# One encoder layer on one core: the first four rows of x loaded together with their weights, three output tiles in one pass, the last product's banks primed with the residual, and the copies of turned probabilities tied

## The chip, the cores and the metric

The kernel runs on 1 core of one Trainium2 chip. The metric is the time of one execution on the device in microseconds (us). The times of a kernel are the median of its runs; a profile is one further execution with the hardware profiler on.

## The reference

One layer over 512 positions of width 2048, in float32. With `xn = rms_norm(x)`:

```
proj = xn @ w_in                    # 2048 x 5120: u_val, u_gate, q, k, v
y_conv = silu(layer_norm(depthwise_conv31(u_val * sigmoid(u_gate))))
y_na   = softmax(q k / 8 + bias) v  # 16 heads of 64, window 8 x 16 on an 8 x 64 grid
x = x + [rms_norm(y_conv), rms_norm(y_na)] @ w_out
up = depthwise_conv3(rms_norm(x) @ w_up);  gate, val = split(up)      # 2 x 5632
x = x + (silu(gate) * val) @ w_down
out = rms_norm(x)
```

## The kernel before

Every matrix product is made at more than half precision of float32 from two rounded parts: a weight tile `raw` is copied by ScalarE (ACT) to a high part `whi` (L133), and VectorE (DVE) makes the low part `wlo = raw - whi` (L134). The activations are split in the same way (`xh`, `xl`). One block of 128 x 128 weights then costs three matmuls over 512 positions: hi x hi, hi x lo, lo x hi (L150, L151, L153). `parts` makes the pair and keeps four of each (NW = 4); `weights` (L172) hands out the next pair and keeps three made ahead (AHEAD = 3). A pair is a "unit" of 8 blocks, so 24 matmuls.

The work of TensorE (PE) runs in this order:

- **Filler.** 11 matmuls on a tile of ones (WARM, L122), which the profile counts as 22.
- **First GLU** (`first_glu`, L357). The value and gate tiles of channel block 0, side by side in two banks, while x comes in. The weights for this come in an order of their own, `w_0`: for each of the 16 rows of x (128 channels by 512 positions), the two blocks that it multiplies. Rows 0 and 1 are loaded alone on SyncE's queue (SP, L289), and their weights on ScalarE's queue (L109), together with the factors `g1` (L104). Later rows come in pairs (L294), and their weights in pieces of 2 or 4 rows (`cuts`, `piece`). `split_x` makes `xh` and `xl` with the factor of the norm on ACT (L270) and DVE (L271). `pin` keeps these instructions in the order written. Behind this stage x is loaded again with positions on the partitions (`xn`, L306) for the sums of squares (L312).
- **Projections.** Channel blocks 1 to 7 (two tiles each) and 8 pairs of heads (three tiles each), mixed by ORDER. Behind them DVE runs the 31 taps of the depthwise convolution, at most four behind each `wlo`. `attend` makes a pair's attention as steps, of which `tick` runs one behind each unit: scores, softmax, then `turn` (TensorE turns the probabilities, L517, bank `trp`), `turned_p` (ACT copies them out as `pt`, L525), then `values` (L534, in the bank `po`). The convolution branch is finished during head pairs 5 and 6; its last root is made in the bank `po` too, and ACT copies it out as `ra` (L254).
- **Output product, gated MLP** (L641 to L860): as a seven-product scheme over halves.
- **Last product** (`product2`, L874), seven products over `TURN2`, four banks each. The last is c = 5 for output rows 0 to 255 and columns 0 to 1023. Its last four units are held back (TAIL), and each bank is finished by itself. Then `ready` (L930) adds the bank to `e3`, the residual with all earlier products (L936), squares it on ACT (L938) and multiplies by the last norm's factor (L940); `all_but_one` and `write` make the root and scale and store the rows.

A scheduler chooses the order of the instructions on each engine by priorities in the order of the program; `shifted` moves a priority, and `issue_after(i)` puts what it holds behind the instruction i.

Of the kernel before, what the change touches and what calls it, by code (L numbers as in the profile page):

```python
# [16 lines left out]
P = 128  # L17
# [17 lines left out]
U = 8  # L35
# [14 lines left out]
WARM = 11  # L50
# [26 lines left out]
def layer(ctx: ExitStack, tc: tile.TileContext, xT, xn, w_0, w_in, w_out, w_up, w_down, par, tab, g3, out):  # L77
# [26 lines left out]
    nc.scalar.dma_start(g1, par[:, :KD])  # L104
    cuts = (0, 1, 2, 4, 8, 12, 16)
    first = []
    for k0, k1 in zip(cuts[:3], cuts[1:4]):
        first.append(t2("we")[:, :2 * (k1 - k0) * P])
        nc.scalar.dma_start(first[-1], w_0[:, 2 * k0 * P:2 * k1 * P])  # L109
# [20 lines left out]
    def parts(raw, n):  # L130
        hi = wpool.tile([P, U * P], F32R, tag="whi", name="whi", bufs=NW)
        lo = wpool.tile([P, U * P], F32R, tag="wlo", name="wlo", bufs=NW)
        i = nc.scalar.activation(hi[:, :n], raw[:, :n], AF.Copy)  # L133
# [10 lines left out]
    tight, taps = [], []  # L144
# [123 lines left out]
    def split_x(k, x):  # L268
        h, l = t2("xh", F32R), t2("xl", F32R)
        pin(nc.scalar.activation(h, x, AF.Copy, scale=g1[:, k:k + 1]))  # L270
        pin(nc.vector.scalar_tensor_tensor(l, x, g1[:, k:k + 1], h.bitcast(F32), op0=ALU.mult, op1=ALU.subtract))  # L271
        xs.append((h, l))

    def piece(raw, k0, k1):
        if k1 - k0 > 2:
            raw, i = raw_unit(w_0[:, 2 * k0 * P:2 * k1 * P], 2 * (k1 - k0) * P)
            pin(i)
            w = parts(raw, 2 * (k1 - k0) * P)
        else:
            w = t2("weh", F32R)[:, :2 * (k1 - k0) * P], t2("wel", F32R)[:, :2 * (k1 - k0) * P]  # L280
            w += nc.scalar.activation(w[0], raw, AF.Copy), nc.vector.tensor_sub(w[1], raw, w[0].bitcast(F32))
        pin(w[2])
        pin(w[3])
        return k0, k1, w[0], w[1]

    pieces, early = [], []
    for k in range(2):
        x = t2("x")
        pin(nc.sync.dma_start(x, xT[0][:, k * S:(k + 1) * S]))  # L289
        split_x(k, x)  # L290
        pieces.append(piece(first[k], k, k + 1))
    for p, at in ((1, 2), (2, 3), (3, 0), (4, 4), (5, 0), (6, 5), (7, 0)):
# [4 lines left out]
        if at:  # L297
            pieces.append(piece(first[2] if at == 2 else None, cuts[at], cuts[at + 1]))
    squares = sm.tile([P, S // P, 2], F32, tag="ss", name="ss")
    for u in range(2):  # L300
        raw, i = raw_unit(w_in[NC_ + 1, :, u * U * P:(u + 1) * U * P], U * P)
        pin(i)
        for t in range(2 * u, 2 * u + 2):
            for i in range(2):
                x = t4([P, D // 2], "xn")
                pin(nc.sync.dma_start(x, xn[t * P:(t + 1) * P, i * D // 2:(i + 1) * D // 2]))  # L306
                if t == 2 * u and i == 0:
                    w = parts(raw, U * P)
                    pin(w[2])
                    pin(w[3])  # L310
                    early.append(w[:2])
                pin(nc.scalar.activation(x, x, AF.Square, accum_out=squares[:, t, i:i + 1]))  # L312
    last = pin(nc.sync.dma_start(prm, par))
    for i in range(6):
        plan.append(lambda i=i: early[i - 4] if i > 3 else None)
# [6 lines left out]
    del plan[6:12]  # L322
# [5 lines left out]
    def stats1():  # L328
        for _ in range(3):
# [20 lines left out]
    ys, ypair = [], []  # L350

    def glu(i):
        pg, pv = project(NC_ + i), project(i)
# [3 lines left out]
    def first_glu():  # L357
        two = [psa.tile([P, S], F32, tag="tr", name="pj", bufs=2) for _ in range(2)]
        for n, (k0, k1, hi, lo) in enumerate(pieces):
            if n > 1:  # L360
                weights()
            for k in range(k0, k1):
                for x in range(2):
                    for i, ps in enumerate(two):
                        o = (2 * (k - k0) + i) * P
                        nc.tensor.matmul(ps, hi[:, o:o + P], xs[k][x], start=k == x == 0, stop=False)  # L366
            for k in range(k0, k1):
                for i, ps in enumerate(two):
                    o = (2 * (k - k0) + i) * P
                    m = nc.tensor.matmul(ps, lo[:, o:o + P], xs[k][0], start=False, stop=k == KD - 1)  # L370
            if n > 1:
                tick(m)
        late.append(lambda: gated(0, *two))
# [93 lines left out]
    def attend(p, q, ks, v):  # L467
# [53 lines left out]
        def turned_p(two):  # L521
            for ps in two:
                pt = t2("pt").rearrange("p (c k) -> p c k", c=4)
                with shifted(-SOONER):
                    nc.scalar.activation(pt, ps, AF.Copy)  # L525
                pts.append(pt)

# [402 lines left out]
    def ready(x, ps, th, dh, only=range(2 * Q), fused=()):  # L930

        for i in only:
# [3 lines left out]
            add(x[i], x[i], ps[i])  # L936
            q = t2("sq")
            nc.scalar.activation(q, x[i], AF.Square, accum_out=sq[th][:, t, o:o + 1])  # L938
            if i not in fused:
                nc.vector.tensor_mul(x[i], x[i], gs[d])  # L940
# [9 lines left out]
    def write(th, t, ys, most=None, fused=()):  # L950
# [8 lines left out]
        for d in reversed(range(Q)):  # L959
            for dh in range(2):  # L960
# [4 lines left out]
                elif i in fused:  # L965
                    nc.vector.scalar_tensor_tensor(x, x, y, gs[d], op0=ALU.mult, op1=ALU.mult)
# [33 lines left out]
    a = four(True)  # L1000
# [75 lines left out]
```

## Time and profile before

| | |
|---|---|
| median of 3 runs | 1975.71 us (1975.62 to 1977.12) |
| the profiled execution | 1976.0 us |
| its span, first to last instruction | 1974.2 us |
| busy: PE, PEld, DVE, ACT, POOL | 99%, 84%, 82%, 56%, 11% of the span |
| HBM read and written | 430.27 MB and 111.15 MB |

The profiled execution's own time is 1.8 us above its span and 0.3 us above the median. The profile names an instruction by engine, line of the kernel and tile: "PE pj L366" is a matmul of TensorE that line 366 issues into the tile `pj`. PEld is the loading of weights into the array, which runs beside the matmuls. "ACTq" and "SPq" are the engines' sequencers when they issue transfers. A matmul's shown duration overlaps with the next one's, so the pace is read from starts, or from the chain of waits, which counts each piece of time once.

### The profile page before, as it was taken

The page shows a single profiled execution, that of the slowest core. Times are in us where ns is not written, and L with a number is a line of the kernel's source. Part 1 is how long each engine was busy: PE and PEld are TensorE (multiplying, and loading weights), DVE is VectorE, ACT ScalarE, POOL GpSimd, SP SyncE. Part 2 cuts the span into 40 slices and gives each one's busy share as a digit, 9 for nine tenths or more (in the row PEclk, how much of TensorE's full clock was granted, in tenths as well). Part 3 has the DMA queues.
Part 4 walks back from the last instruction along what each step waited for, and adds up shares of the span by engine and source line. Part 5 has one row for each costly group of instructions (what it writes and reads, how often), then busy time and mean ns, then how long its engine had stood idle before and what let it go on. Part 6 is the DMA issues. An engine that isn't in the chain of part 4 may idle for free.

```text
span 1974.2 us, 27655 instructions
## 1 busy us (share of the span) xinstructions
PE 1960.6 (99%) x10141; PEld 1668.0 (84%) x10141; DVE 1611.7 (82%) x2338; ACT 1105.8 (56%) x1750; POOL 225.7 (11%) x310
## 2 busy tenths in 40 slices
PE   9999999999999999999999999999999999999998
PEld 7888888888788888888888888888888888888886
DVE  5987688787547888888989898988888898886765
ACT  6244424548525666666666666666666654554654
POOL 0111111111001111111111111111110400000000
PEclk9999999999999999999999999999999999999999
DMA  9776767766758889999999999999986977665663
GB/s 369 186 204 177 189 184 193 181 192 215 254 139 216 207 237 267 248 260 259 249 261 249 265 246 272 245 268 242 268 225 177 377 243 233 222 213 192 192 202 118
DMA packets 141817, 450.98 MB, mean 228 GB/s; under 512 B 15088, under 2 KB 23536, under 8 KB 140272
## 3 DMA queue, kind: packets, MB, share of 16 engines
q1 hardware_dynamic: 88880, 293.46, 43.8%
q0 software_dynamic: 42624, 148.92, 35.0%
q10 hardware_dynamic: 10176, 6.83, 1.1%
q8 instruction: 80, 1.31, 0.3%
q14 instruction: 57, 0.47, 0.1%
HBM read 430.27 MB, written 111.15 MB: 274 GB/s over the span
## 4 chain that ended last, share of the span: by engine, by line
PE 98%; DVE 1%; ACT 0%; DMA 0%; issue 0%; ACTq 0%; DVEq 0%
PE pu L746 43%; PE pd L885 21%; PE pj L150 7%; PE pj L151 7%; PE pj L153 7%; PE po L150 3%; PE po L151 3%; PE po L153 3%; PE po L534 1%; PE sc L488 1%; PE trp L517 1%; PE pj L366 1%; DMA we<-in_w 0%; PE trx L641 0%; PE pj L370 0%; DVE acc L407 0%
## 5 line engine op out<-in xcount | busy, mean ns | idle before, releaser
L133 ACT ACTIVATE whi<-raw 128x1024 fp32r<-128x1024 f32 x573 | 604.8, 1057 | 563.7 <-PE pj L151 166.6
L134 DVE TENSOR_TENSOR wlo<-raw,whi 128x1024 fp32r<-128x1024 f32 x573 | 699.5, 1222 | 232.5 <-ACT whi L133 192.0
L746 PE MATMUL pu<-xc,whi 128*128 128x512 f32 x2464 | 593.6, 391 | 0.0
L746 PEld LDWEIGHTS pu<-xc,whi 128*128 128x128 f32 x2464 | 451.3, 188 | 86.8 <-DVE xc L634 0.4
L746 PEld LDWEIGHTS pu<-xc,wlo 128*128 128x128 f32 x2464 | 319.2, 191 | 13.7
L746 PE MATMUL pu<-xc,wlo 128*128 128x256 f32 x2464 | 324.2, 283 | 0.0
L885 PE MATMUL pd<-whi,ho 128*128 128x512 f32 x1232 | 305.0, 389 | 0.1
L885 PEld LDWEIGHTS pd<-whi,ho 128*128 128x128 f32 x1232 | 231.1, 188 | 48.7 <-DVE vl L759 0.5
L150 PE MATMUL pj<-xh,whi 128*128 128x512 f32 x608 | 239.0, 393 | 0.0
L151 PE MATMUL pj<-xl,whi 128*128 128x512 f32 x608 | 236.9, 390 | 0.0
L392 DVE SCALAR_TENSOR_TENSOR y<-ch,prm,y 128x500 f32<-128x500 f32 (+14 forms) x240 | 177.3, 742 | 5.3
L885 PE MATMUL pd<-wlo,ho 128*128 128x512 f32 x616 | 165.1, 389 | 0.0
L153 PE MATMUL pj<-xh,wlo 128*128 128x512 f32 x608 | 150.3, 389 | 0.0
L150 PEld LDWEIGHTS pj<-xh,whi 128*128 128x128 f32 x608 | 114.1, 188 | 26.7 <-issue 2.8
L885 PEld LDWEIGHTS pd<-wlo,ho 128*128 128x128 f32 x616 | 115.6, 188 | 24.1
L153 PEld LDWEIGHTS pj<-xh,wlo 128*128 128x128 f32 x608 | 114.1, 188 | 23.7
L151 PEld LDWEIGHTS pj<-xl,whi 128*128 128x128 f32 x608 | 114.2, 188 | 23.6 <-issue 0.2
L755 ACT ACTIVATE pu<-pu 128x512 f32<-128x512 f32 x132 | 76.5, 580 | 92.9 <-PE pu L746 92.9
L695 POOL DMA_DIRECT2D raw<-in_w_up x88 | 78.0, 887 | 357.8 <-DVE wlo L134 206.7
L205 POOL DMA_DIRECT2D ws<-in_w_down x88 | 79.8, 907 | 309.1 <-DMA ws<-in_w_down 123.2
L202 POOL DMA_DIRECT2D ws<-ws x44 | 23.0, 524 | 318.1 <-PE pj L153 105.9
L202 POOL DMA_DIRECT2D ws<-in_w_down x44 | 22.9, 520 | 312.8 <-PE pj L153 172.9
(189 smaller groups left out, 1980.6 us busy)
## 6 DMA issues: line engine op xcount, KB each, us to landing
raw<-in_w_up SPq DMA_DIRECT2D x220, 512.0 KB, 5.9
ws<-in_w_down POOLq DMA_DIRECT2D x132, 512.0 KB, 6.1
raw<-in_w_up POOLq DMA_DIRECT2D x88, 512.0 KB, 7.4
raw<-ws SPq DMA_DIRECT2D x88, 512.0 KB, 4.2
raw<-in_w_in SPq DMA_DIRECT2D x76, 512.0 KB, 5.2
raw<-in_w_down SPq DMA_DIRECT2D x66, 512.0 KB, 3.8
ws<-ws POOLq DMA_DIRECT2D x44, 512.0 KB, 5.8
raw<-in_w_out SPq DMA_DIRECT2D x32, 512.0 KB, 5.3
```

The lines of the kernel that those rows point to most:

```text
L133: i = nc.scalar.activation(hi[:, :n], raw[:, :n], AF.Copy)
L134: j = nc.vector.tensor_sub(lo[:, :n], raw[:, :n], hi[:, :n].bitcast(F32))
L150: nc.tensor.matmul(ps, hi, mh, start=first and k == 0, stop=False)
L151: nc.tensor.matmul(ps, hi, ml, start=False, stop=False)
L153: i = nc.tensor.matmul(ps, lo[:, wk * P:(wk + 1) * P], mh, start=False, stop=last and k == len(ws) - 1)
L202: behind(nc.gpsimd.dma_start(wsum[c][k], a), ins)
L205: nc.gpsimd.dma_start(wsum[c][k], w_down[k, {1: A21, 2: A11, 4: A11, 6: A12}[c]], accum_op=ALU.add, max_dma_last_dim=ROW)
L392: nc.vector.scalar_tensor_tensor(y[:, a:b], h[:, a + j - PAD:b + j - PAD], prm[:, o:o + 1], y[:, a:b], op0=ALU.mult, op1=ALU.add)
L695: nc.gpsimd.dma_start(a[c], w_up[f, q2], accum_op=ALU.add)
L746: i = nc.tensor.matmul(ps[:, :n], part[:, k * P:(k + 1) * P], comb[c][k][:, :n], start=j == 0 and not more, stop=j == 2 * U - 1, skip_grou ...
L755: nc.scalar.activation(to, ps, AF.Copy)
L885: m = nc.tensor.matmul(ps[i], h[:, o + t * P:o + (t + 1) * P], w[:, d], start=start and not more and kind == 0 and j == 0, stop=stop and k ...
```

## The change

1. **Start.** For rows 0 to 3 the host packs one array `xw`: a row of x, its three weight blocks, and (used in row 0 alone) the factors `g1`. One transfer on SP brings each row, 128 x 912 or 128 x 896 values. ACT's queue issues no transfer in the beginning. In row 0 ACT and DVE share the making of the high parts. Rows 4 to 15 come in six pairs, each with its piece of weights (128 x 768).
2. **Three tiles side by side.** `w_0` holds three blocks per row: gate 0, value 0 and gate 1. `first_glu` makes 9 matmuls per row of x and not 6, and the next channel block then makes its value tile alone. The number of matmuls of the layer stays. The third tile takes a bank of `psm`. `gated(0)` is called directly behind, and not through `late`.
3. **Filler.** WARM is 8 and not 11.
4. **Squares.** The loads of `xn` stand one behind each pair from row 6 on, with the rest behind it, and not all at the end.
5. **Tie.** `turned_p` leaves its last copy in `copies`, and the next `parts` puts its ACT copy behind it.
6. **Last product.** `prime` has ACT copy `e3` into the four banks before product c = 5 starts; the product adds to it (`product2(5, primed, True)`). `ready` then squares and multiplies from the bank and has no addition. In `write` the fused block reads the bank, and d runs upward.

```diff
-WARM = 11
+WARM = 8
+ROWS = 4
...
     def parts(raw, n):
...
-        i = nc.scalar.activation(hi[:, :n], raw[:, :n], AF.Copy)
+        with tc.issue_after(copies.pop().ins) if copies else nullcontext():
+            i = nc.scalar.activation(hi[:, :n], raw[:, :n], AF.Copy)
...
+    for k in range(ROWS):
+        n = 3 * P
+        both = t4([P, S + n + KD], "xw")
+        m = S + n + (0 if k else KD)
+        pin(nc.sync.dma_start(both[:, :m], xw[k][:, :m]))
+        x, raw, lo = both[:, :S], both[:, S:S + n], t2("wel", F32R)[:, :n]
+        if k:
+            split_x(k, x)
+            his = [t2("weh", F32R)[:, :n]]
+            pin(nc.scalar.activation(his[0], raw, AF.Copy))
...
+            pin(nc.scalar.activation(h[:, :H], x[:, :H], AF.Copy, scale=g))
+            pin(nc.vector.tensor_copy(his[0], raw[:, :P]))
+            pin(nc.vector.tensor_scalar(h[:, H:], x[:, H:], g, None, op0=ALU.mult))
+            pin(nc.scalar.activation(his[1], raw[:, P:], AF.Copy))
+            pin(nc.vector.tensor_copy(g1, both[:, S + n:]))
+            pin(nc.vector.scalar_tensor_tensor(l, x, g, h.bitcast(F32), op0=ALU.mult, op1=ALU.subtract))
...
+    for p in range(ROWS // 2, KD // 2):
         x = t4([P, 2 * S], "x")
         pin(nc.sync.dma_start(x, xT[p]))
         for k in range(2):
             split_x(2 * p + k, x[:, k * S:(k + 1) * S])
...
+        piece(2 * p, 2 * p + 2)
+        if p > 2:
+            square(*todo.pop(0))
...
     def glu(i):
-        pg, pv = project(NC_ + i), project(i)
+        pg = gate.pop() if gate else project(NC_ + i)
+        pv = project(i)
...
-        two = [psa.tile([P, S], F32, tag="tr", name="pj", bufs=2) for _ in range(2)]
+        three = [psa.tile([P, S], F32, tag="tr", name="pj", bufs=2) for _ in range(2)]
+        three.append(psm.tile([P, S], F32, tag="mm", name="pj"))
...
-        late.append(lambda: gated(0, *two))
+        gate.append(three[2])
+        gated(0, *three[:2])
...
-                    nc.scalar.activation(pt, ps, AF.Copy)
+                    i = nc.scalar.activation(pt, ps, AF.Copy)
                 pts.append(pt)
+            copies[:] = [i]
...
-            add(x[i], x[i], ps[i])
+            if not whole:
+                add(x[i], x[i], ps[i])
+            src = ps[i] if whole else x[i]
...
+    def prime(x):
+        primed.extend(four(True))
+        for a, b in zip(x, primed):
+            nc.scalar.activation(b, a, AF.Copy)
+            yield
...
-        for d in reversed(range(Q)):
+        for d in range(Q):
...
-                    nc.vector.scalar_tensor_tensor(x, x, y, gs[d], op0=ALU.mult, op1=ALU.mult)
+                    nc.vector.scalar_tensor_tensor(x, primed[i], y, gs[d], op0=ALU.mult, op1=ALU.mult)
...
-    steps += [ready(e0, a, 0, 1), ready(e1, a, 1, 1)]
+    steps += [ready(e0, a, 0, 1), ready(e1, a, 1, 1), prime(e3)]
     run(6, b, True)
...
-    for i in product2(5, a, False):
+    for i in product2(5, primed, True):
         with shifted(-100):
-            for _ in ready(e3, a, 0, 0, (i,), fused):
+            for _ in ready(e3, primed, 0, 0, (i,), True, fused):
                 pass
```

The lines of the changed kernel have numbers of their own: L129 is the old L133 (`whi`), L130 the old L134, L545 the old L525, L250 the old L254, L385 and L389 the old L366 and L370, L906 the old L885.

**The first instructions of ACT**, before. `x` is a row of x, `we` its weights, `g_76` the factors:

```order
L104 DMA g_76<-in_par 128x16
L109 DMA we<-in_w 128x256 x2
L109 DMA we<-in_w 128x512
L119 ACT_TABLE_LOAD
L119 ACTIVATE idle<-ones 128x1
L270 ACTIVATE xh<-x,g_76 128x512
L281 ACTIVATE weh<-we 128x256
```

And of the changed kernel, where `xw` holds both:

```order
L114 ACT_TABLE_LOAD
L114 ACTIVATE idle<-ones 128x1
L303 ACTIVATE xh<-xw 128x256
L306 ACTIVATE weh<-xw 128x256
L267 ACTIVATE xh<-xw,g_76 128x512
```

Four transfers have left ACT's queue, and the first row's high parts are half as long on ACT, since DVE makes the other half.

**ACT at the end of head pair 6's turn**, where the convolution branch's last root `ra` is copied, before:

```order
L237 ACTIVATE rsr<-rsv 128x4
L133 ACTIVATE whi<-raw 128x1024 x4
L525 ACTIVATE pt<-trp 128x512 x4
L254 ACTIVATE ra<-st 128x512
L572 ACTIVATE ao<-po 128x512
```

And of the changed kernel:

```order
L233 ACTIVATE rsr<-rsv 128x4
L129 ACTIVATE whi<-raw 128x1024
L545 ACTIVATE pt<-trp 128x512 x4
L250 ACTIVATE ra<-st 128x512
L129 ACTIVATE whi<-raw 128x1024 x3
L593 ACTIVATE ao<-po 128x512
```

Three of the four copies of weights have moved behind the four copies of turned probabilities and behind `ra`. At the other head pairs one or two copies of weights move behind the four `pt` in the same way. From the projections to the last four units of the last product, PE's own order is what it was, except that the two matmuls of the first root (L252) stand in the second unit behind the first GLU and not in the third.

**The last instructions of DVE**, before (the last bank, from its addition on):

```order
L936 TENSOR_TENSOR xr<-xr,pd 128x512
L955 TENSOR_SCALAR rsv<-sq,rsm 128x1
L956 SCALAR_TENSOR_TENSOR rsv<-rsr,rsv 128x1
L957 RECIPROCAL rsv<-rsv 128x1
L958 TENSOR_SCALAR rsy<-rsv,rsr 128x1
L966 SCALAR_TENSOR_TENSOR xr<-xr,rsy,g_15502 128x512
L968 TENSOR_SCALAR xr<-xr,rsy 128x512
```

And of the changed kernel:

```order
L986 TENSOR_SCALAR rsv<-sq,rsm 128x1
L987 SCALAR_TENSOR_TENSOR rsv<-rsr,rsv 128x1
L988 RECIPROCAL rsv<-rsv 128x1
L989 TENSOR_SCALAR rsy<-rsv,rsr 128x1
L999 TENSOR_SCALAR xr<-xr,rsy 128x512
L997 SCALAR_TENSOR_TENSOR xr<-pd,rsy,g_15509 128x512
```

The addition is gone, and the plain scaling stands ahead of the fused one, which reads the bank `pd`.

More of the change, by code (lines that the diff above doesn't have):

```diff
@@ L1 @@
-from contextlib import ExitStack, contextmanager
+from contextlib import ExitStack, contextmanager, nullcontext
 import numpy as np
@@ L103, in layer @@
     g1 = consts.tile([P, KD], F32, name="g1")
[L104 to L109, printed above, removed]
     def pc(name, i):
@@ L286, in layer, with piece @@
[L286 to L292, printed above, removed]
+    def piece(k0, k1):
+        n = 3 * (k1 - k0) * P
+        raw, i = raw_unit(w_0[:, 3 * k0 * P:3 * k1 * P], n)
+        pin(i)
+        w = parts(raw, n)
+        for i in w[2:]:
+            pin(i)
+        pieces.append((k0, k1, [w[0]], w[1]))
@@ L328, in stats1 @@
     def stats1():
-        for _ in range(3):
+        for _ in range(2):
             yield
@@ L928, in taken, with ready @@
             yield
-    def ready(x, ps, th, dh, only=range(2 * Q), fused=()):
+    def ready(x, ps, th, dh, only=range(2 * Q), whole=False, fused=()):
         for i in only:
```

89 lines of the change are left out of this document (45 added, 44 removed).

## The prediction

> **What bounds the kernel now.** I began with the page's busy times and its chain.
>
> ```profile
> PE 1960.6 (99%) x10141; PEld 1668.0 (84%) x10141; DVE 1611.7 (82%) x2338; ACT 1105.8 (56%) x1750; POOL 225.7 (11%) x310
> PE 98%; DVE 1%; ACT 0%; DMA 0%; issue 0%; ACTq 0%; DVEq 0%
> ```
>
> TensorE is 98% of the chain that ended last, so a change that leaves its matmuls alone can only win where TensorE stands still. The change leaves their number alone. How much standing is there? The waits of TensorE come next (total, times, longest), then the last stretches of the span by engine.
>
> ```profile
> PE po L534 <- ACT ra L254: 1.9, 1, 1.9
> PE pj L366 <- ACT weh L281: 1.4, 3, 0.7
> PE warm L122 <- DVE ones L117: 1.1, 1, 1.1
> PE st L410 <- DVE acc L407: 0.3, 1, 0.3
> ...
> 1965.00:1970.00 5.00, 0.45 (x2) 0.02 (x1) 3.37 (x11) 2.92 (x6) 0.00 (x0) 0.94 0.60 221
> ```
>
> Three places hold nearly all of it: the beginning up to the last wait for `weh`, one wait of 1.9 us in the middle, and 8.75 us from 1965.45 to the end at 1974.2, where TensorE has nothing left. They are the three places that the change touches. Each is sized alone, since TensorE works without a gap between them.
>
> **The start.** The timeline of TensorE and ACT, with start, duration, and in brackets the idle time before and its releaser:
>
> ```profile
> 0.75 0.86 SPq L289 DMA_DIRECT2D x<-in_xT  x2
> 1.06 5.06 PE L122 MATMUL warm<-ones 128*128 128x128 f32 x22 [1.06 <-DVE ones L117]
> 4.04 0.72 ACT L270 ACTIVATE xh<-x,g 128x512 fp32r<-128x512 f32 x1
> 6.06 0.42 ACT L281 ACTIVATE weh<-we 128x256 fp32r<-128x256 f32 x1 [1.30 <-DMA we<-in_w]
> 6.53 0.82 PE L366 MATMUL pj<-xh,weh 128*128 128x512 f32 x2 [0.41 <-ACT weh L281]
> 7.18 0.62 PE L366 MATMUL pj<-xl,weh 128*128 128x512 f32 x2
> 10.93 0.73 PE L366 MATMUL pj<-xh,weh 128*128 128x512 f32 x2 [0.31 <-ACT weh L281]
> 13.77 0.62 PE L366 MATMUL pj<-xh,whi 128*128 128x512 f32 x2
> ...
> 13.93 3.63 PE pj L366 x16
> ```
>
> The last row is of the chain: 16 matmuls in 3.63 us, 0.227 each. By 13.77 the 12 of rows 0 and 1 and the 12 of rows 2 and 3 are done, 24 x 0.227 = 5.45 us of work. So TensorE stands as if it had begun at 13.77 - 5.45 = 8.32 and never waited. That is the number to beat. What is late is not x but its weights, which come on ACT's queue beside the rows of x on SP's (the transfers issued in the first 1.2 us with their median time to landing, then the landings of `x` issued in the first 5 us, then a stretch in which the transfers run full):
>
> ```profile
> x<-in_xT SPq DMA_DIRECT2D x2, 256.0 KB, 3.3
> we<-in_w ACTq DMA_DIRECT2D x1, 128.0 KB, 4.8
> ...
> DMA to landing us min/median/max: 3.1/4.8/7.4
> ...
> 20.00:30.00 10.00, 10.00 (x46) 8.29 (x45) 4.35 (x6) 7.13 (x12) 0.00 (x0) 1.00 1.02 391
> ```
>
> A row of x (256 KB) lands 3.3 us after its issue, 128 KB of weights on the other queue 4.8. The changed kernel has one queue and one transfer of 128 x 912 values, 456 KB. No such transfer is in the trace. From the rows: issued at 0.75 it lands no earlier than x does now with all its rivals, 0.75 + 3.1 = 3.85 (3.1 is the first row's), and with 200 KB more at 391 GB/s, 0.5 us, at 4.4. I take 3.9, the early end, as the small transfers of ACT's queue are gone. Then ACT's half of the row takes the 0.42 of a 128 x 256 copy; DVE's rounding of 128 x 128 and its half of the row are not in the trace, and 0.2 to 0.6 together bounds them by the same 0.42. First matmul possible at 4.5, at worst 5.0.
>
> TensorE itself is free when the filler ends: 21 starts in 5.06 - 0.42 us (the last one shows 0.42), 0.221 each, so 16 records from 1.06 end at 4.6. So the start is set by the filler and not by the load, just so. Behind it nothing is late: a row now costs TensorE 9 x 0.227 = 2.04 us, its transfer of 448 KB 1.17 at 391 GB/s, ACT 0.72 and about 0.53 for 384 columns, DVE as much. A pair from row 6 on costs TensorE 4.08, the transfers 1408 KB, 3.7 us, `xn` included. Up to the last `xn` 12.3 MB are moved, 32 us, so the squares end near 35 us, and the root's matmuls stand 172 matmuls in, at 44. That is the point of three tiles side by side: before, a row held 6 matmuls, 1.36 us, and the late pieces of weights stopped TensorE three times.
>
> One cost comes back. The first two matmuls at 6.53 take 0.82 where the next two take 0.62: the first still ran at about half pace, as did the filler, and TensorE came to its full pace near 6.7. If that moment stays, matmuls from 4.6 to 6.7 run at half pace and (6.7 - 4.6) / 2 = 1.05 us are lost. The effective beginning is 4.6 + 1.05 = 5.65 and the **gain 8.32 - 5.65 = 2.67 us**. Bounds: 3.7 with no slow stretch, 2.0 if the full pace comes later by what the three dropped filler matmuls filled, 6 x 0.221 = 1.3 us, as it would if TensorE's own work were counted.
>
> The Trainium skill ("TensorE: Matmul & The Clock Gate", section "What's actually happening") says that the clock is released after one busy window of 3.4 us, and that the windows run freely. By that rule the release lies anywhere from 4.5 to 7.9 with work from 1.06 on, an estimate from that page, and the gain from 3.7 to 2.05. The trace has one such moment, 6.7, which fits; the sum above uses only that one.
>
> **The middle.** ACT and TensorE around the 1.9 us wait; the last two rows are TensorE's:
>
> ```profile
> 493.32 1.99 ACT L133 ACTIVATE whi<-raw 128x1024 fp32r<-128x1024 f32 x2
> 506.71 1.06 ACT L133 ACTIVATE whi<-raw 128x1024 fp32r<-128x1024 f32 x1 [4.38 <-PE po L151]
> 507.79 2.06 ACT L525 ACTIVATE pt<-trp 128x512 f32<-128x512 f32 x4
> 509.72 0.63 ACT L254 ACTIVATE ra<-st 128x512 f32<-128x512 f32 x1
> 495.22 1.91 PE L517 MATMUL trp<-ident,s 128*128 128x128 f32 x16
> 510.40 1.97 PE L534 MATMUL po<-pt,vt 128*64 128x128 f32 x32 [1.92 <-ACT ra L254]
> ```
>
> The turned probabilities are ready at 497.13, but ACT's queue has a `whi` first that must wait until TensorE frees a buffer at 506.7. So `pt` and `ra` come 10 us late and L534 waits for `ra`. With the tie only one `whi` stands ahead: `pt` runs from 497.1 to 499.2 and `ra` to 499.8, while TensorE comes to L534 at 508.5. The wait has 8.7 us of room, so **all 1.92 us go**. What is late next? The three `whi` behind `ra`, and DVE's `wlo` behind them. The second starts at about 499.8 and not 494.3. But each of four buffers is refilled as soon as TensorE has left it and read again three units later, 3 x 24 x 0.227 = 16.3 us, so 5.5 us are covered. The same cover holds at the other seven pairs. The wait for `acc` (L410) stays: DVE's order before it is unchanged.
>
> **The end.** TensorE's last matmuls, then the chain behind them:
>
> ```profile
> 1964.38 1.07 PE L885 MATMUL pd<-wlo,ho 128*128 128x512 f32 x4
> 1965.73 0.68 DVE L936 TENSOR_TENSOR xr<-xr,pd 128x512 f32<-128x512 f32 x1
> 1966.44 0.63 ACT L938 ACTIVATE sq<-xr 128x512 f32<-128x512 f32 x1 [0.87 <-DVE xr L936]
> 1967.98 0.21 DVE L958 TENSOR_SCALAR rsy<-rsv,rsr 128x1 f32<-128x1 f32 x1
> 1968.98 0.95 ACTq L970 DMA_DIRECT2D out_T<-xr  x2
> ...
> L525 ACT ACTIVATE pt<-trp x32: 592/603/621, 137.6 to 539.3; 128x512 f32<-128x512 f32 x32
> ```
>
> TensorE ends at 1965.45; DVE, held up by earlier scaling, adds at 1965.73, and ACT squares at 1966.44. Now ACT squares from the bank, at about 1965.5: **0.94 us earlier**. Reading a bank costs ACT no more: its copies of 512 columns from banks take 0.603, the square from SBUF 0.63. Behind the square the chain is the same in length. Of the two last scalings of DVE only the order changes. Bounds: 0.7 (the addition alone) and 1.1 (the first store leaves 0.27 earlier, and the stores share the engines). The four copies of `prime` are about 2.4 us of ACT in a stretch where ACT is half idle, and DVE loses four additions there. TensorE's order among the last four units changes so that seven matmuls and not four (1.6 us) cover the time until the first half of the double bank is read; the square and the multiplication take 0.63 and 0.69, so the 0.1 us that is lost there now stays.
>
> **The sum.** 2.67 + 1.92 + 0.94 = 5.53 us. The span falls from 1974.2 to 1968.7, the profiled time from 1976.0 to 1970.5; the median lies 0.3 below that execution, so I predict 1970.2 us, 0.28% faster. The measurement can tell about 0.2%, 3.95 us, from no change, so the line is at 1971.76.
>
> **The rivals.**
>
> *The pace comes late.* The full pace came 5.7 us after the filler began. If the shorter filler or a gap of some tenths behind it starts that count anew at 4.6, the pace comes at 10.3, (10.3 - 4.6) / 2 = 2.85 are lost, the beginning is 7.45 and the gain there 0.87: 1972.0 us. Against it: the gap of 0.41 at 6.53 did no harm. Chance 0.07.
>
> *The load is as slow as the rows of x on the whole.* The view of all transfers of the span has this for them, with the median time to landing last:
>
> ```profile
> x<-in_xT SPq DMA_DIRECT2D x18, 256.0 KB, 7.4
> ```
>
> Landing at 0.75 + 7.4 = 8.15 and a row 0 with its waits would begin effectively at about 9, after the 8.32 of now: -0.7 for +2.67, so 1973.6 us. Against it: those 18 stand behind other traffic, and this one is first. Chance 0.07.
>
> *The change doesn't do what it says in the middle.* The wait moves to the next reader, say to DVE's addition behind a late `wlo`, and stays 1.92 us: 1972.1 us. The order speaks against it. Chance 0.06.
>
> *Slower.* The tie makes a `whi` wait for `pt`, and `pt` waits for TensorE's turn. If the cover of three units is not there, because the schedule puts the tied `whi` just before its reader, TensorE waits for four `pt` and a `whi`, 2.06 + 1.06 = 3.1 us, at each of 8 pairs: 25 us, less 5.5, 1995 us. It decides when a tied `whi` comes more than 16 us later than now; the one I could follow comes 5.5 us later. Chance 0.05.
>
> **Chances and range.** The forecast has 0.75, with a range of its own from 1969.0 (3.7 + 1.92 + 1.1) to 1971.5 (2.0 + 1.5 + 0.7). Taking in the first and third rival, and 0.2 us for the spread of executions, the range is 1968.8 to 1972.1. Faster by over 0.2%: 0.75; within: 0.20 (the first three rivals); slower: 0.05.
>
> **What would show it.** In the changed profile: the first real matmul at 4.6 to 5.0 and no wait for `weh` over 0.2 us behind row 0; the end of the first GLU (144 matmuls) at 38.3, where now 96 end at 30.1; L534 of pair 6 with no wait; the square of the last bank within 0.1 us of the last matmul; no new row of more than 1 us among TensorE's waits. I am wrong if TensorE waits for transfers between rows 1 and 15, if its matmuls up to 10 us run at half pace, or if the scores and values of other pairs show new waits for `whi`.

## The result and the profile after

The changed kernel takes 1970.51 us (median of 8 runs, 1970.19 to 1971.00); the kernel before took 1976.07 us beside it (8 runs, 1975.62 to 1977.61). The ratio is 0.9970, with a 95% interval of 0.9961 to 0.9979: faster by 0.3%. Predicted were 1970.2 us and a range of 1968.8 to 1972.1. The profiled execution took 1970.35 us, with a span of 1968.6 where before had 1974.2.

The busy times and the chain of the page after:

```profile
PE 1958.6 (99%) x10135; PEld 1666.7 (85%) x10135; DVE 1610.5 (82%) x2340; ACT 1106.6 (56%) x1756; POOL 225.4 (11%) x310
PE 98%; DVE 1%; issue 0%; DMA 0%; ACT 0%; DVEq 0%
```

TensorE is busy 2.0 us less, with six filler records fewer. It is still 98% of the chain, so what was won was standing time. The waits of TensorE after (total, times, longest), all of 0.2 us or more:

```profile
PE warm L117 <- DVE ones L112: 1.1, 1, 1.1
PE st L430 <- DVE acc L427: 0.3, 1, 0.3
```

The rows for `ra` (1.9) and `weh` (1.4) are gone and no row has come in their place. The timeline after, at the three places: TensorE and ACT at the start, then around head pair 6, then the last work of TensorE and what follows it.

```profile
1.06 3.79 PE L117 MATMUL warm<-ones 128*128 128x128 f32 x16 [1.06 <-DVE ones L112]
4.33 0.51 ACT L303 ACTIVATE xh<-xw 128x256 fp32r<-128x256 f32 x1 [2.08 <-DMA xw<-in_xw]
4.96 0.96 PE L385 MATMUL pj<-xh,weh 128*128 128x512 f32 x3
5.76 0.94 PE L385 MATMUL pj<-xl,weh 128*128 128x512 f32 x3
6.54 0.85 PE L389 MATMUL pj<-xh,wel 128*128 128x512 f32 x3
13.35 0.84 PE L385 MATMUL pj<-xh,whi 128*128 128x512 f32 x3
...
493.13 2.06 ACT L545 ACTIVATE pt<-trp 128x512 f32<-128x512 f32 x4 [1.93 <-PE trp L537]
495.06 0.63 ACT L250 ACTIVATE ra<-st 128x512 f32<-128x512 f32 x1
503.34 1.98 PE L149 MATMUL po<-mah,wlo 128*128 128x512 f32 x8
505.25 1.97 PE L555 MATMUL po<-pt,vt 128*64 128x128 f32 x32
...
1959.21 1.07 PE L906 MATMUL pd<-wlo,ho 128*128 128x512 f32 x4
1960.32 0.60 ACT L961 ACTIVATE sq<-pd 128x512 f32<-128x512 f32 x1 [0.76 <-PE pd L906]
1961.82 0.21 DVE L989 TENSOR_SCALAR rsy<-rsv,rsr 128x1 f32<-128x1 f32 x1
1962.82 0.95 ACTq L1001 DMA_DIRECT2D out_T<-xr  x2
```

**Start.** The 37th matmul starts at 13.35; less 36 x 0.227 = 8.17, TensorE stands as if it had begun at 5.18. Before it was 8.32, so the gain is 3.14. Real matmuls ran at full pace almost at once: the second group of three starts 0.80 behind the first, the third 0.78 behind the second, where full pace is 0.68; the rest is the wait for `xl` of row 0 and slower first matmuls behind the waits. **Middle.** `ra` is copied at 495.06, 10.2 us before L555 needs it. The eight `wlo` matmuls from 503.34 need 8 x 0.227 = 1.82, so L555 could start at 505.16 and did at 505.25: 0.09 lost. Before, 2.08 were lost there in the same reckoning (a wait of 1.92 and some slower starts), so the gain is 1.99. **End.** The last matmul ends at 1960.28 and the square starts 0.04 later. The span goes on for 8.31 us behind that matmul; before it was 8.78, so the gain is only 0.47. Together 3.14 + 1.99 + 0.47 = 5.60; the spans differ by 5.6.

So two parts gave more than I forecast and one gave half. The first GLU (144 matmuls) ends at 37.8, where 38.3 was forecast. The experiments ask where the half went, and how much of the start belongs to which edit.

### The profile page after: what moved, and what is told of

Its sections match the earlier page's. It is cut to its first block, busy times and chain, and to the rows that moved or that the text cites. A ratio compares the mean times of both kernels' runs of the same rounds, so it can differ in the third digit from the quotient of the medians.

```text
span 1968.6 us, 27654 instructions
## 1 busy us (share of the span) xinstructions
PE 1958.6 (99%) x10135; PEld 1666.7 (85%) x10135; DVE 1610.5 (82%) x2340; ACT 1106.6 (56%) x1756; POOL 225.4 (11%) x310
## 3 DMA queue, kind: packets, MB, share of 16 engines
q10 hardware_dynamic: 9600, 6.29, 1.1%
## 4 chain that ended last, share of the span: by engine, by line
PE 98%; DVE 1%; issue 0%; DMA 0%; ACT 0%; DVEq 0%
PE pu L767 44%; PE pd L906 21%; PE pj L146 7%; PE pj L147 7%; PE pj L149 7%; PE po L146 3%; PE po L147 3%; PE po L149 3%; PE pj L385 1%; PE po L555 1%; PE sc L508 1%; PE trp L537 1%; PE pj L389 1%; PE trx L662 0%; DVE acc L427 0%
## 5 line engine op out<-in xcount | busy, mean ns | idle before, releaser
L129 ACT ACTIVATE whi<-raw 128x1024 fp32r<-128x1024 f32 (+1 forms) x574 | 604.7, 1055 | 539.5 <-PE pj L147 146.0
L130 DVE TENSOR_TENSOR wlo<-raw,whi 128x1024 fp32r<-128x1024 f32 (+1 forms) x574 | 699.1, 1219 | 232.5 <-ACT whi L129 195.8
L906 PE MATMUL pd<-whi,ho 128*128 128x512 f32 x1232 | 305.1, 389 | 0.1
L906 PEld LDWEIGHTS pd<-whi,ho 128*128 128x128 f32 x1232 | 231.1, 188 | 48.7 <-DVE vl L780 0.5
L146 PE MATMUL pj<-xh,whi 128*128 128x512 f32 x592 | 232.7, 393 | 0.0
L147 PE MATMUL pj<-xl,whi 128*128 128x512 f32 x592 | 230.7, 390 | 0.0
L906 PE MATMUL pd<-wlo,ho 128*128 128x512 f32 x616 | 165.1, 389 | 0.0
L149 PE MATMUL pj<-xh,wlo 128*128 128x512 f32 x592 | 146.3, 389 | 0.0
L906 PEld LDWEIGHTS pd<-wlo,ho 128*128 128x128 f32 x616 | 115.6, 188 | 24.1
```

Of the source, the lines that this page charges most:

```text
L146: nc.tensor.matmul(ps, hi, mh, start=first and k == 0, stop=False)
L147: nc.tensor.matmul(ps, hi, ml, start=False, stop=False)
L149: i = nc.tensor.matmul(ps, lo[:, wk * P:(wk + 1) * P], mh, start=False, stop=last and k == len(ws) - 1)
L906: m = nc.tensor.matmul(ps[i], h[:, o + t * P:o + (t + 1) * P], w[:, d], start=start and not more and kind == 0 and j == 0, stop=stop and k ...
```

## The experiments

Each kernel was timed beside the kernel before; changes are against the median of before beside it (1975.84, 1976.12 or 1976.20 us). The changed kernel itself stands at -5.56.

**The three parts alone.** The tie in the kernel before:

```diff
-        i = nc.scalar.activation(hi[:, :n], raw[:, :n], AF.Copy)
+        with tc.issue_after(copies.pop().ins) if copies else nullcontext():
+            i = nc.scalar.activation(hi[:, :n], raw[:, :n], AF.Copy)
...
+            copies[:] = [i]
```

> The kernel before with part 5 alone, the tie. Theory: the 1.92 us wait of L534 for ra goes and nothing else moves, so 2.0 us less, 0.999 of before, and no row of TensorE's waits above 0.5 us behind the start. Rival (the wait went because the earlier start shifted the schedule): the wait stays near 1.9 us and the time is that of before. Rival (a tied copy of weights comes too late for its reader): new waits at the other seven pairs, slower than before.

Measured: 1973.94 us (1973.75 to 1974.28), -1.90; ratio 0.9988 (0.9979 to 0.9998). In its waits the row for `ra` is gone and nothing has replaced it.

The primed banks in the kernel before:

```diff
+    steps += [ready(e0, a, 0, 1), ready(e1, a, 1, 1), prime(e3)]
...
-    for i in product2(5, a, False):
+    for i in product2(5, primed, True):
...
-            add(x[i], x[i], ps[i])
+            if not whole:
+                add(x[i], x[i], ps[i])
```

> The kernel before with part 6 alone, the banks of the last product primed. The square of the last bank should start 0.05 us behind the last matmul, where before it is 0.99. Theory A (the stores of the first 128 rows still hold the transfer engines when the last stores come): from the last matmul to the end 8.3 us where before it is 8.8, so 0.5 us less. Theory B (the late last landing in the changed kernel's profile is chance): 7.8 us, 0.94 less.

Measured: 1974.82 us (1974.29 to 1976.50), -1.02; ratio 0.9993 (0.9983 to 1.0003). The interval holds 1, so the time alone does not show the gain; the reading rests on the trace. There the square starts 0.04 behind the last matmul, and the span ends 7.55 us behind it. That is 1.23 less than before, more than the 0.95 by which the square came forward, and less than either theory said (8.3 and 7.8).

The new start (edits 1 to 4) in the kernel before, shown against the changed kernel, from which the tie and the primed banks are taken out:

```diff
-    for i in product2(5, primed, True):
+    for i in product2(5, a, False):
...
-        with tc.issue_after(copies.pop().ins) if copies else nullcontext():
-            i = nc.scalar.activation(hi[:, :n], raw[:, :n], AF.Copy)
+        i = nc.scalar.activation(hi[:, :n], raw[:, :n], AF.Copy)
```

> The kernel before with parts 1 to 4 alone, the start. Theory: the three places are independent, TensorE begins effectively at 5.2 us and not at 8.3, 3.1 us less; the waits in the middle (1.9 us) and the end (8.8 us from the last matmul) stay as they were. Rival (the gain is partly given back by DVE's taps, which begin later against TensorE): a longer wait for acc at L430 and less than 2.5 us.

Measured: 1973.87 us (1973.49 to 1976.05), -1.97; ratio 0.9991 (0.9982 to 1.0000), at the edge of the noise. This missed its number. The effective beginning is 5.27, 3.05 sooner, as expected; but the wait for `acc` grew from 0.3 to 0.6, and the span ends 9.37 us behind the last matmul, 0.59 later than in the kernel before. 3.05 - 0.3 - 0.59 = 2.16, which is what the spans differ by (1974.2 and 1972.07). No edit of this kernel touches the end, and its stores are issued at the same times behind the last matmul as before (last one 4.14 us). Only their landing is later: 8.27 us behind the last matmul and not 7.66. The view of the tile `out_T` over its 16 stores, before and with the new start alone:

```profile
DMA to landing us min/median/max: 2.2/3.5/7.0
...
DMA to landing us min/median/max: 2.4/4.1/7.8
```

So **a change at the start lengthens the end**, and the changed kernel has that too: 8.31 where the primed banks alone gave 7.55.

**Without the tie**, the rest kept:

```diff
-        with tc.issue_after(copies.pop().ins) if copies else nullcontext():
-            i = nc.scalar.activation(hi[:, :n], raw[:, :n], AF.Copy)
+        i = nc.scalar.activation(hi[:, :n], raw[:, :n], AF.Copy)
```

> The changed kernel without the tie: the rounding of the weights may again go ahead of the copies of the turned probabilities on ScalarE. Theory (the wait of pair 6 is worth its length wherever the program begins): the matmul of 'po' behind 'ra' waits 1.9 us again, nothing before or behind it moves, 1970.5 + 1.9 = 1972.4 us. Rival (with the earlier start the order around pair 6 is another, and part of the wait is taken by waits that were there anyway): a wait under 1 us, 1970.5 to 1971.5 us.

Measured: 1972.83 us (1972.50 to 1975.12), -3.29; ratio 0.9983 (0.9974 to 0.9991). Two of its waits of TensorE:

```profile
PE po L553 <- ACT ra L249: 1.9, 1, 1.9
...
PE st L429 <- DVE acc L426: 0.6, 1, 0.6
```

The same 1.9 us came back, wherever the program begins, and the rival falls. The wait for `acc` is 0.6 as with the new start alone, and 0.3 with the tie, so in the changed kernel the tie takes out 0.3 us more. It is worth 1.9 to 2.3 us in both kernels.

The spread of the times shows one thing more. Of the 134 executions of kernels with the wait for `ra` (the kernel before each time, the primed banks, the new start, the shifted kernel before and this one), 45 took over 1.4 us more than the fastest of their kernel, and on the mean 1.4 to 2.3 us more than the others of their kernel. Of the 59 executions without the wait (the two kernels with sixteen loads below left out) none did. Where the runs list a granted clock, those executions have 0.9979 on the mean and the others 0.9987. One stretch of 3.4 us at half clock, as the trace with sixteen loads has it below, would be 0.0009 of the clock and 1.7 us. So the wait probably costs such a stretch in a third of the executions, and the tie takes that out too; no kept trace is of such an execution, so this is not shown.

**The filler.** Back to 11, and halved to 4:

```diff
-WARM = 8
+WARM = 11
```

> The changed kernel with the filler of before, 11 and not 8. The filler's 22 records end at about 5.75 and the first row is there at 4.3. Theory (TensorE's pace depends on how long it has worked, and the load and not the filler sets the beginning at 8): the first real matmul comes at 5.8 to 5.9 and not 4.96, 0.8 to 0.9 us more than the changed kernel, all matmuls at full pace. Rival (the filler sets the beginning): 1.28 us more, the length of six records.

```diff
-WARM = 8
+WARM = 4
```

> The changed kernel with half of the filler: 8 matmuls on ones instead of 16, so the filler ends near 2.9 us of the span instead of 4.8, and TensorE stands idle for about 2 us until the first joined row has landed (4.30 in the changed kernel, first real matmul at 4.96). Theory A: the begin is set by that load alone, and the time is the changed kernel's, 1970.5 us within 0.3. Rival B: the granted clock is full from 4.88 us in the changed kernel only because the filler ran up to it; with the idle stretch the real matmuls begin at half pace and full clock comes 1 to 3 us later, which costs half of that: 1971.0 to 1972.0 us, and the row of the granted clock by stretch shows it.

Measured: with 11 1970.73 us (1970.24 to 1971.59), -5.11; ratio 0.9974 (0.9964 to 0.9985). With 4 1971.85 us (1971.54 to 1972.84), -4.27; ratio 0.9976 (0.9967 to 0.9985). The timeline of TensorE with 4:

```profile
1.06 2.07 PE L117 MATMUL warm<-ones 128*128 128x128 f32 x8 [1.06 <-DVE ones L112]
4.83 1.62 PE L385 MATMUL pj<-xh,weh 128*128 128x512 f32 x3 [1.69 <-DVE g L307]
6.24 1.48 PE L385 MATMUL pj<-xl,weh 128*128 128x512 f32 x3
7.52 1.48 PE L389 MATMUL pj<-xh,wel 128*128 128x512 f32 x3
8.80 0.99 PE L385 MATMUL pj<-xh,weh 128*128 128x512 f32 x3
```

The groups of three stand 1.41, 1.28 and 1.28 apart: half pace until 9.06, where the trace has the change of the clock. Theory A of that run (the load alone sets the begin) falls. The first matmul came at the same time, but TensorE begins effectively at 6.90 and not at 5.18, 1.7 us later in the profile and 1.3 in the median. So between 4 and 8 the filler's length matters not for when row 0 can start but for the pace at which it runs. With 11 the filler ends late: the first real matmul comes at 5.78, and the effective beginning of the profiled execution is 6.08, 0.9 later than in the changed kernel. The medians differ by less (0.45, with overlapping intervals); the pace comes at another moment in each execution, as follows below.

**Joining the rows, and the third tile.** First the weights of rows 0 to 3 as transfers of their own on ACT's queue:

```diff
+        nc.scalar.dma_start(boths[k][:, S:m], xw[k][:, S:m])
...
-        pin(nc.sync.dma_start(both[:, :m], xw[k][:, :m]))
+        pin(nc.sync.dma_start(both[:, :S], xw[k][:, :S]))
```

> The changed kernel with the three tiles side by side, but the four rows not joined: x of a row comes on SyncE's queue and its weights on ScalarE's, as two transfers. Theory A (joining matters): the two transfers of row 0 share the queue engines with those of rows 1 to 3, whose weights are issued at once on the second queue; the later of the two lands after the 4.30 us of the joined row, the first real matmul comes after 4.96 by 0.3 to 1.0 us, and TensorE waits for 'weh' or 'g1': 1970.8 to 1971.5 us. Rival B (only the bytes count): the first real matmul at 4.7 to 5.1 us, 1970.5 us within 0.3.

Measured: 1970.82 us (1970.48 to 1971.01), -5.38; ratio 0.9971 (0.9959 to 0.9982). Row 0 landed at 3.98 and its weights at 4.16, the first matmul started at 4.81, TensorE begins effectively at 5.04, and no wait for `weh` appears. Theory A falls: joining the rows gives nothing that shows here. Then two tiles side by side, the joined rows kept:

```diff
-        n = 3 * P
+        n = 2 * P
...
-        three.append(psm.tile([P, S], F32, tag="mm", name="pj"))
...
-        gate.append(three[2])
```

> The changed kernel with two tiles side by side as before, the joined rows kept. In the changed kernel the joined rows land 1.1 to 1.5 us apart (4.30, 5.74, 6.86, 8.00) and one row is 9 matmuls, 2.04 us at 0.227; with two tiles a row is 6 matmuls, 1.36 us, and smaller by a third of its weights. Theory A (the third tile is there to outlast the loads): TensorE runs into the loads again, with waits for 'weh', 'whi' or 'xh' of 0.5 to 2 us in all in the first 25 us: 1971.0 to 1972.5 us. Rival B (joining alone brought the gain): no wait over 0.2 us behind row 0, 1970.5 us within 0.3.

Measured: 1973.14 us (1972.48 to 1973.76), -3.06; ratio 0.9983 (0.9974 to 0.9992): 2.5 us of the gain are gone. Its timeline of TensorE, the first matmuls of the later pairs of rows:

```profile
4.59 1.19 PE L384 MATMUL pj<-xh,weh 128*128 128x512 f32 x2
...
19.75 0.73 PE L384 MATMUL pj<-xh,whi 128*128 128x512 f32 x2 [0.21 <-ACT whi L129]
...
22.98 0.73 PE L384 MATMUL pj<-xh,whi 128*128 128x512 f32 x2 [0.22 <-ACT whi L129]
...
26.23 0.74 PE L384 MATMUL pj<-xh,whi 128*128 128x512 f32 x2 [0.24 <-ACT whi L129]
...
29.45 0.50 PE L146 MATMUL pj<-xh,whi 128*128 128x512 f32 x1 [0.17 <-ACT whi L129]
```

Row 0 starts sooner, at 4.59, yet the pairs come 3.23 us apart, where 12 matmuls need 2.72. A pair moves 512 KB of `x`, 256 KB of weights and 512 KB of `xn`; in 3.23 us that is 406 GB/s, which is also what the transfers of this trace moved from 16.61 to 29.45. Each pair is late by 0.5 us. With the third tile a pair costs TensorE 4.08 and moves 1408 KB, 3.6 us at that rate, so the loads keep ahead. By the 97th matmul the effective beginning has moved to 7.66. Theory A holds in kind, though the waits cost more than it said (its range ended at 1972.5): **the third tile carries most of the gain of the start**, 2.5 of 3.1 us, as it makes TensorE the slower of the two.

**The lengthened end.** Two suspects. One is where the output lies in memory, since the inputs have grown by 2.78 MiB. The other is a transfer of 8 KB of instructions, which the trace shows among the last stores of the changed kernel. All transfers from 1966.18 to 1966.78, 5.9 to 6.5 us behind the last matmul (queue, kind, packets, MB, share):

```profile
q10 hardware_dynamic: 40, 0.06, 24.9%
q14 instruction: 1, 0.01, 3.2%
q1 hardware_dynamic: 5, 0.00, 0.5%
```

First the place alone, with rows that nobody reads: 356 of zeros behind `xn` in the kernel before, and 156 in the changed kernel.

```diff
-    "xn": np.ascontiguousarray(a["x"][0])
+    "xn": np.concatenate([a["x"][0], np.zeros((356, D), np.float32)])
```

> The kernel before, instruction for instruction, with 356 rows of zeros that nobody reads behind the array 'xn', 2,916,352 bytes, as much as the changed kernel's inputs are larger than before's. It asks why the last stores landed 8.27 us behind the last matmul with the new start alone and 7.66 us in the kernel before, at the same times of issue. Theory A: where the output lies in memory sets how fast its stores land; then this kernel's last store lands 0.6 us later than before's, 8.2 to 8.3 us behind the last matmul, and the time rises by 0.6 to 1976.4 us. Rival B: it is something of the new start's instructions (their tiles or their transfers); then the last store lands 7.6 to 7.7 us behind the last matmul and the time is before's, 1975.8 us.

> The changed kernel, instruction for instruction, with 156 rows of zeros that nobody reads behind the array 'xn', so that its inputs are 4 MiB larger than before's instead of 2.78. Theory A (the place of the output in memory sets how fast its stores land, and a round step brings back before's place): the last store lands 6.4 us behind the last matmul, as with the primed banks alone, instead of 7.20, and the time falls by 0.8 to 1969.7 us. Rival B (the instructions of the new start do it): 7.2 us, 1970.5 us. A landing that is later than 7.2 us would speak for A too, with a place that is worse.

Measured: the shifted kernel before 1975.95 us (1975.21 to 1977.67), -0.17, ratio 0.9999 (0.9990 to 1.0008); the shifted changed kernel 1970.87 us (1970.21 to 1971.33), -5.25, ratio 0.9971 (0.9959 to 0.9982). No time moved by what theory A said. The landings did move. In the kernel before, the first four of the last eight stores landed 0.28 to 0.49 us later with the shift (1.72, 2.53, 3.37, 4.05 us behind the last matmul instead of 1.43, 2.25, 2.91, 3.56); the last one, at 7.84, was only 0.18 later. In the changed kernel the first seven landed 0.27 to 0.57 sooner; the last did not (7.19 and 7.20). The view of the tile `out_T` shows it over all 16 stores. In the changed kernel:

```profile
DMA to landing us min/median/max: 2.5/3.9/7.8
```

And in the changed kernel with the shift:

```profile
DMA to landing us min/median/max: 2.2/3.7/7.4
```

So the place slows the stores but does not set the end alone. In the shifted changed kernel the transfer of instructions ran from 6.02 to 6.33 us behind the last matmul, and the last packet of a store started at 6.33, as that transfer ended; the packet before it had ended at 6.04. The next two kernels are to move that transfer away: 16 loads of one number each on SP's queue make SyncE's code longer.

```diff
+    scrap = consts.tile([1, 16], F32, name="scrap")
+    for i in range(16):
+        pin(nc.sync.dma_start(scrap[:, i:i + 1], par[:1, i:i + 1]))
```

> The changed kernel with 16 loads of one number each on SyncE's queue behind the parameters, at some 28 us, which nobody reads. It asks for the second half of what the end gave back: in the changed kernel a transfer of 8 KB of instructions ran 6.04 to 6.34 us behind the last matmul, among the last stores, and the last packet of the stores ran behind it; with the primed banks alone it ran at 7.21, when all had landed. SyncE has 1247 instructions in the changed kernel and 1241 with the primed banks alone. Theory A (it is SyncE's code, and the place of its blocks moves with the count of its instructions): with 16 more the transfer comes 16 instructions sooner, ahead of the stores; the last store lands 6.7 to 6.9 us behind the last matmul instead of 7.20, and the time falls by 0.3 to 0.5, to about 1970.1 us. Rival B (another engine's code): the transfer stays at 6.04 and the last landing at 7.20; 1970.5 us.

> The changed kernel with the 16 loads and with the 156 unread rows of zeros behind 'xn'. With the rows alone the first seven of the last eight stores landed 0.3 to 0.6 us sooner than in the changed kernel, and only the last one, behind the transfer of instructions, at 7.19. Theory A (both causes together make up the 0.8 us between this end and that of the primed banks alone): the last store lands 6.4 us behind the last matmul, the span ends 7.5 us behind it instead of 8.3, and the time is 1969.7 us, the best of all. Rival B: one of the two is not the cause, and the span ends 7.9 us or more behind the last matmul, 1970.1 us or more.

Measured: with the loads 1975.04 us (1974.47 to 1975.97), -1.16, ratio 0.9993 (0.9984 to 1.0002); with the loads and the rows 1974.63 us (1973.53 to 1975.79), -1.57, ratio 0.9989 (0.9980 to 0.9998). As times both are misses by some 5 us, and at another place. The loads were not free. The timeline of SyncE's issues in the kernel with the loads:

```profile
28.40 11.07 SPq L333 DMA_DIRECT2D scrap<-in_par  x16
39.57 19.93 SPq L123 DMA_DIRECT2D raw<-in_w_in  x11
```

Its longest wait of TensorE:

```profile
PE pj L146 <- ACT whi L129: 3.2, 1, 3.2
```

And three stretches around that wait, busy time of PE, PEld, DVE, ACT and POOL, then the granted clock, the share of the DMA engines and GB/s:

```profile
52.00:52.40 0.40, 0.00 (x0) 0.00 (x0) 0.30 (x2) 0.40 (x2) 0.00 (x0) 1.00 0.60 246
...
53.00:54.00 1.00, 1.00 (x4) 0.81 (x3) 1.00 (x1) 1.00 (x2) 0.00 (x0) 0.50 0.08 16
...
56.00:57.00 1.00, 1.00 (x6) 0.83 (x5) 0.96 (x2) 0.00 (x0) 0.00 (x0) 0.94 0.86 258
```

Sixteen loads of 4 bytes held SyncE for 11 us, since each waited for the semaphore of the transfer eight places before it. The weights behind them came late, TensorE stood for 3.2 us, and the granted clock was 0.50 from 52.70 to 56.11, which cost another 1.6 us (the first nine matmuls took 3.76 us, where the nine behind the wait at 29.45 of the two-tile trace took 2.18).

The end of these kernels, which is what they were made for, came out as theory A said. Behind the last matmul, from the traces:

| kernel | last transfer of SyncE's instructions starts | last packet of a store ends | span ends |
|---|---|---|---|
| before | 8.74 | 7.31 | 8.78 |
| primed banks alone | 7.21 | 6.04 | 7.55 |
| new start alone | 6.74 | 7.79 | 9.37 |
| changed | 6.04 | 6.43 | 8.31 |
| changed, place moved | 6.02 | 6.41 | 8.29 |
| changed, code moved | -35.30 | 6.29 | 7.84 |
| changed, both | -34.64 | 6.04 | 7.49 |

Each row is one profiled execution; the traces with a filler of 11, of 4 and without the tie have the changed kernel's end again (8.29 to 8.32). Moving the place alone gave 0.02 us, as the last packet waited behind the transfer anyway; moving the code alone gave 0.47, both 0.82. With both the end is that of the primed banks alone (7.49 and 7.55). Of the 0.47, only 0.14 is the last packet; the rest is its landing, which came 0.77 us behind that packet where the transfer ran just ahead of it (the rows "changed" and "place moved") and 0.35 to 0.48 in the others. Why the landing is late there is not shown.

That the transfer is SyncE's code can be read from the traces: in all 14 the last one starts when SyncE has 1231 to 1238 records behind it (the trace keeps three fewer than the instructions counted above), be that 35 us ahead of the last matmul or 8.7 behind it. The counts of ScalarE, VectorE and TensorE at that moment differ by 40 and more between traces, and GpSimd issues nothing from 96 us ahead of the last matmul until the program closes. The kernel before and the primed banks alone have 1238 records of SyncE, so the transfer comes at their very end; the new start brings 1244, and the transfer moves in among the last stores. The kernel with two tiles has 1248 and no added loads; its transfer ran at 4.59, and its span ended 7.99 us behind the last matmul. What it is about the place that slows a store was not tried. Nor was a version that moves both without holding SyncE; by the end of the last row it would be some 0.8 us below the changed kernel, an estimate.

## Why the prediction was right

The three places held, and so did what each edit does there, but the sum, 5.53 forecast and 5.60 measured, is closer than its terms: the start gave 0.47 more and the end 0.47 less, and that these cancel is luck.

- **Start, 2.67 forecast, 3.14 measured.** The step "so the start is set by the filler and not by the load, just so" failed: the row landed at 4.3 and not at 3.9, TensorE was free at 4.6 and stood until 4.96. That cost 0.4. The step "if that moment stays, matmuls from 4.6 to 6.7 run at half pace" failed too, the other way: in this execution the full pace came at 4.88, ahead of the first real matmul, and of the 1.05 only 0.2 were lost, at row 0's waits. That the pace is not tied to a moment shows in other traces with the filler from 1.06 on: it came, among others, at 4.00 (no tie), 4.39 (two queues), 5.47 (new start alone), 6.20 (filler of 11), 6.53 (shifted changed kernel), 6.73 (before) and 7.29 (shifted kernel before). The estimate from the Trainium skill ("TensorE: Matmul & The Clock Gate", section "What's actually happening") was 4.5 to 7.9, and the gain 2.05 to 3.7; these executions agree with a freely running window, but for two that lie up to 0.5 us ahead of it. The gain is less loose than that. In the seven traces with the new start, the filler of 8 and three tiles, TensorE begins effectively between 5.04 and 5.89, five times by 5.3; in the four with the old start between 7.80 and 8.59. So some 3 us is the usual gain, and 2.67 was too low since 6.7, the one moment that the trace before had, is a late one. The rival in which the pace starts anew did not occur with a filler of 8. With 4, where TensorE waited for 1.7 us behind the filler, something like it did: the full pace came 4.2 us behind the first real matmul.
- **That rows 1 to 15 would keep ahead of TensorE** held, and for the reason given, as the run with two tiles shows. That joining the transfers helps was no step of the sum, and it did not. The reading that the weights were late as they came on ACT's queue beside x is not borne out: on two queues they landed at 4.16. In the kernel before, the factors' transfer stood ahead of them and they were issued at 1.19; which of the differences made them late was not tried.
- **Middle, 1.92 forecast, 1.99 measured.** All steps held: `pt` before `ra` before the three `whi`, room of about 9 us (9.6 us from the end of `ra` to L555), no new wait for `whi` at any pair. The rivals with the tie, the wait that moves on and the starving by pairs, did not occur.
- **End, 0.94 forecast, 0.47 measured.** The square moved by 0.95, as forecast. The step that failed is "behind the square the chain is the same in length". It is, up to the last issue (3.15 us behind the square before, 3.11 after); from there to the end it was 4.64 us before and 5.16 after. 0.8 us were taken by the place of the output and the transfer of instructions, both moved by edits elsewhere; the prediction had no term for either. Without them the primed banks are worth 1.23, more than the upper bound of 1.1; the first half of the last stores is issued 0.6 to 0.8 us sooner, which is probably the rest.

## What to carry to other kernels

When loads and TensorE run side by side at the start, compare bytes per row with matmuls per row: here a third tile on the same data did what joining the transfers did not. A wait that an in-order queue makes (copies for later ahead of copies for now) can be taken out whole by one tie, if the buffers behind it are refilled early enough. Compare the spread of the times too, and not only their medians: a short wait may cost more than its length in some executions. Count what is behind the last matmul to the last landing, not to the last issue, and try a changed kernel's end with its arrays shifted, and see when each engine's code is fetched, before crediting or blaming an edit for a few tenths.

## What the runs showed of the hardware

- A start of the full pace between 4.00 and 7.29 us with the same filler from 1.06, in executions of nearly the same code; and a wait of 3.2 us in mid-program enough to bring half pace back for 3.4 us, 0.3 and 1.1 us after the matmuls had gone on (two traces). The Trainium skill ("TensorE: Matmul & The Clock Gate", section "HAM oscillation — how this bites in real kernels") names gaps over about 3.4 us; the gap here was shorter, so 3.4 is not a safe limit.
- Packets of 2 KB of the last eight stores took 96 ns on the mean in the changed kernel and 88 ns with the output's place moved by 1.2 MiB.
- An 8 KB transfer of SyncE's instructions took 0.31 us, and, in the changed kernel with the output's place moved, the last packet of the stores started only as it ended, 0.29 us after the packet before it had ended.
- Sixteen loads of one number on a queue with full transfers ahead: 1.28 us from one issue to the next for the first six, and 11 us for all.
